# A hybrid attention and state-space layer on one core: the first pairs' products in another order, and norms, table load and splits queued in another place

## The chip, the cores and the metric

The kernel runs on one core of a Trainium2 chip. The metric is the device time of one execution in microseconds. A core has TensorE (PE in the profile, its weight loads PEld), VectorE (DVE), ScalarE (ACT), GpSimd (POOL) and SyncE (SP), which issues most of the transfers. Each engine works through its own queue in order and waits on semaphores for the others.

## The reference

One decoder layer on x of 1024 rows by 1024 columns, float32. What matters here is the head of it: the normalised input and one combined projection.

```python
def _rmsnorm(x, g):
    xf = x.astype(jnp.float32)
    y = xf * lax.rsqrt(jnp.mean(xf * xf, axis=-1, keepdims=True) + RMS_EPS) * g.astype(jnp.float32)
    return y.astype(x.dtype)
...
    h = _rmsnorm(x, pre_g)
    proj = jnp.einsum('bld,de->ble', h, w_in)
    z_ssm, xbc, dt_raw, q, k, v, f_raw, z_att, g_ssm, g_att = jnp.split(proj, _offsets(IN_SPLITS), axis=-1)
```

A state-space branch and an attention branch follow, are gated and merged, go through `w_out`, are normalised and added to x. The change touches none of these.

## The kernel before

Every large product is done in pairs of 128 output columns, by a scheme of seven half-size products in place of eight. A `Pair` holds two column tiles of weights, each in two halves of rows (`a11`, `a12`, `a21`, `a22`). `Pair.do(which)` runs product 1 to 7: twelve matmuls of 128x512, three for each of four row tiles, since each operand is kept as a high part (`h`) and the rest (`l`) and h·h, h·l and l·h are added. `OPERAND` names the moving operand of each product: 1 takes `b11` (tiles `x0h`, `x0l`), 2 `b21` (`x1`), 6 `-t2` (`x4`), 5 `t1` (`x3`), 7 `t3` (`x5`), 4 `t4` (`x6`), 3 `-b22` (`x2`). Products 1, 6, 7 and 4 of a pair add up in one PSUM bank (`pb`; p and q, the first two pairs, have one each), 5 and 3 use the bank `pc`, which all pairs share, and 2 uses `pd`. After 1, 6 and 7 ScalarE copies the bank (`s`, L402); `give` (L406 to L416) then makes the four results on VectorE or ScalarE.

`prepare` makes the weights of a product three steps ahead: sums of quarters (`sum`, L355, L371) and the split of a sum or of a raw tile into two parts (`wop`: the high one on ScalarE, L349, the rest on VectorE, L350). The list `Stream.steps` sets the order of products; `half()` runs half of one. Raw tiles (`raw`, six buffers) are loaded through SyncE as soon as the weights made from the old ones are prepared.

Ahead of the stream stands the start (from L1143). Eight tiles of x, 128x1024 each, are loaded. `norm_tiles` squares each (ScalarE, or VectorE for tiles 1 and 3), takes the root on ScalarE (L1175) and the reciprocal on VectorE, and scales the tile: the first four on VectorE (L1178), the other four on GpSimd (L1180). A first loop over eight column blocks turns the first four tiles on TensorE (`pt`), scales them out of PSUM into `low`, and splits `low` into `x0` and `x1` with `put`; from the fifth block on, half a product runs behind each. The second loop has four blocks (j): eight turns of the other four tiles, two copies out of PSUM on ScalarE (`up`, and `b`, both L1225), eight passes of `df` (the columns of dt and f), the differences `t1`, `t2` and their splits `x3`, `x4`, half of a product 2, and two more differences into `low` (L1239, L1240). After it `low` is split into `x5` (`t3`) and `x6` (`t4`), and `b` into `x2` (`-b22`).

`summing` is a small 128x64 matrix by which `df` is turned (`pt_df`), the first work of the state-space stage; behind it a chain of small VectorE operations makes dt (L689 to L713).

What orders this: a scheduler places the instructions of each engine by a timeline of its own. `mm`, `turn` and `pin` keep program order; `tc.high_priority()` puts work ahead; `tc.issue_after(op)` puts it behind `op` on the engine's queue.

Of the kernel before, what the change touches and what calls it, by code (L numbers as in the profile page):

```python
# [16 lines left out]
P = 128  # L17
T = 1024
D = 1024
NK = D // P  # L20
KH = NK // 2
# [65 lines left out]
def hybrid_layer(ctx: ExitStack, tc, a, out):  # L87

    nc = tc.nc
# [5 lines left out]
    ident = const.tile([P, P], F32, name="ident")  # L95
# [6 lines left out]
    epst = const.tile([P, 1], F32, name="epst")  # L102
# [33 lines left out]
    def small(name="th"):  # L136
        return gp.tile([P, HALF], F32, tag="th", name=name)
# [21 lines left out]
    class Operands:  # L159
# [298 lines left out]
    class Stream:  # L458
# [6 lines left out]
        def __init__(self, pairs, double, last):  # L465
            self.pairs = pairs
            for n, p in enumerate(pairs):
                p.bank, p.other = (pj, "be"[n % 2]), (pjx, "d") if n < double else (pj, "c")

                p.between = n < double or n >= last  # L470

            p, q, r = pairs[0:3]
            self.steps = [(p, 1), (q, 1), (p, 2), (q, 2)] + [(p, n) for n in (6, 5, 7, 4, 3)]
            self.steps += [(q, 6), (q, 5), (q, 7), (r, 1), (q, 4), (q, 3)]
            for n in range(2, last):
                p, nxt = pairs[n], pairs[n + 1]
                self.steps += [(p, i) for i in ((2, 6, 5, 7) if n < double else (6, 2, 7, 5))] + [(nxt, 1)]
                self.steps += [(p, 4), (p, 3)] if n + 1 < last else [(p, 3), (p, 4)]

            a, b, c, d, e, f, g, h = pairs[last:]  # L480
            self.steps += [(a, 5), (a, 6), (a, 7), (b, 1), (a, 2), (a, 4), (a, 3)]
            for p, nxt in ((b, c), (c, d), (d, e)):
                self.steps += [(p, 2), (p, 6), (p, 5), (p, 7), (nxt, 1), (p, 4), (p, 3)]
            self.steps += [(f, 1), (e, 2), (e, 6), (e, 5), (e, 7), (f, 2), (e, 4), (e, 3)]
            self.steps += [(f, 6), (f, 5), (f, 7), (g, 1), (f, 4), (f, 3)]
            self.steps += [(g, 2), (g, 6), (g, 5), (g, 7), (h, 1), (g, 4), (g, 3)]
            self.steps += [(h, 6), (h, 5), (h, 7), (h, 2), (h, 3), (h, 4)]
            self.following = {p: n.ops for p, n in zip(pairs, pairs[1:]) if n.ops is not p.ops}
            self.building = []
            self.chores, self.line = [], []  # L490
            self.held = None
            self.count = 0
            self.at = 0
            self.run = None
            self.waiting = []
            self.loads = [(p, names) for p in pairs for names in (("a11", "a12"), ("a21", "a22"))]
            self.loaded = []
            self.load_next()
# [19 lines left out]
        def begin(self):  # L518
            self.load_next()
            self.load_next()  # L520
            for p, which in self.steps[:3]:
                self.prepare(p, which)

        def prepare(self, p, which):
# [69 lines left out]
        def ahead(self, after):  # L594

            if self.at + 3 < len(self.steps):
                p, which = self.steps[self.at + 3]
                if after == (p.keys[0][0] == "merged"):
                    self.prepare(p, which)

# [442 lines left out]
    order = [p for ps in by_group for p in ps]  # L1043
# [100 lines left out]
    with tc.tile_pool(name="pro", bufs=1, reuse_waits="tile", side="right") as pro, tc.tile_pool(  # L1144
        name="prop", bufs=1, space=PSUM, reuse_waits="tile", side="right"
# [5 lines left out]
        ss = pro.tile([P, NT], F32, name="ss")  # L1151
        rstd = pro.tile([P, NT], F32, name="rstd")
        low = pro.tile([P, NK, HALF], F32, name="low")
# [11 lines left out]
                tiles.append(xt)  # L1165
            return tiles

        def norm_tiles(hf, tiles):
            for t, xt in enumerate(tiles, 4 * hf):
                sqt = small("sqt").bitcast(BF16)  # L1170
                if t in (1, 3):
                    nc.vector.tensor_tensor_reduce(sqt, xt, xt, 1.0, 0.0, ALU.mult, ALU.add, ss[:, t : t + 1])
                else:
                    nc.scalar.activation(sqt, xt, AF.Square, accum_out=ss[:, t : t + 1])
                nc.scalar.activation(rstd[:, t : t + 1], ss[:, t : t + 1], AF.Sqrt, bias=epst, scale=1.0 / D)  # L1175
                nc.vector.reciprocal(rstd[:, t : t + 1], rstd[:, t : t + 1])
                if hf == 0:
                    nc.vector.tensor_scalar(xt, xt, rstd[:, t : t + 1], None, ALU.mult)  # L1178
                else:
                    nc.gpsimd.tensor_scalar(xt, xt, rstd[:, t : t + 1], None, ALU.mult)  # L1180

        def turned(tiles, k):
            pt = prop.tile([P, HALF], F32, tag="pt", bufs=2, name="pt")
            for j in range(4):
                turn(pt[:, j * P : (j + 1) * P], tiles[j][:, k * P : (k + 1) * P]) 
            return pt
# [9 lines left out]

        tiles = load_tiles(0)
        stream = Stream(order + late + ends, len(order) + 3, len(order) + len(late) + 4)
        norm_tiles(0, tiles)
        tiles2 = load_tiles(1)  # L1200
        stream.begin()
        for k in range(NK):
            pt = turned(tiles, k)
            if k > 1:
                nc.scalar.activation(low[:, k, :], pt, AF.Copy, scale=preg[:, k : k + 1])
            else:
                nc.vector.tensor_scalar(low[:, k, :], pt, preg[:, k : k + 1], None, ALU.mult)
            put("b11" if k < KH else "b21", k % KH, low[:, k, :])
            if k >= KH:
                stream.halves(1)  # L1210
        norm_tiles(1, tiles2)

        for k, h in [(k, h) for j in range(KH) for k, h in ((j, 0), (j + KH, 0), (j + KH, 1))]:
            pin(nc.sync.dma_start(wo_dram[k, :, half(h)], a["wo"][k * P : (k + 1) * P, half(h)]))
# [1 line left out]
        b22 = []  # L1216
        for j in range(KH):
            up = []
            if j % 2 == 0:
                two = pro.tile([P, D], F32, tag="xt", bufs=6, name="b22")  # L1220
                b22 += [two[:, 0:HALF], two[:, HALF:D]]
            for k in (j, j + KH):
                pt = turned(tiles2, k)
                up.append(b22[j] if k >= KH else pro.tile([P, HALF], F32, tag="up", bufs=1, name="up"))
                nc.scalar.activation(up[-1], pt, AF.Copy, scale=preg[:, k : k + 1])  # L1225
            b11, b21 = low[:, j, :], low[:, j + KH, :]
            for n, (k, m) in enumerate(((j, b11), (j, up[0]), (j + KH, b21), (j + KH, up[1]))):
                mm(df[32 * n : 32 * n + 32, :], wdf[:, k, :], m, start=(j == 0), stop=(j == KH - 1))
            with tc.high_priority():
                t1 = small()  # L1230
                nc.vector.tensor_tensor(t1, up[0], b11, ALU.subtract)
                put("t1", j, t1)
                t2 = small()
                nc.vector.tensor_tensor(t2, up[1], t1, ALU.subtract)
                last = put("-t2", j, t2, -1.0)
            stream.halves(1)

            with tc.issue_after(last[1]) if j == KH - 1 else nullcontext():
                nc.vector.tensor_tensor(b11, t2, b11, ALU.subtract)  # L1239
                nc.vector.tensor_tensor(b21, t2, b21, ALU.subtract)  # L1240
        dft = small("dft")
        nc.scalar.activation(dft, df, AF.Identity, bias=bdf)
        stream.halves(1)
# [1 line left out]
        with tc.issue_after(last[0]), tc.issue_after(last[1]):  # L1245
            for j in range(KH):
                put("t3", j, low[:, j, :], order=pin)
        stream.halves(1)
        early.close()
        pools["t4"] = phase_a.enter_context(tc.tile_pool(name="xp4", bufs=1, reuse_waits="tile"))  # L1250
        xop["t4"] = place(pools["t4"], "t4")
        for j in range(KH):
            put("t4", j, low[:, j + KH, :], order=pin)
        stream.halves(1)
        for j in range(KH):
            put("-b22", j, b22[j], -1.0, order=pin)
        stream.halves(5)


    with tc.tile_pool(name="ssm", bufs=1, reuse_waits="tile", side="right") as sp, tc.tile_pool(  # L1260
        name="ssmp", bufs=1, space=PSUM, reuse_waits="tile", side="right"
# [14 lines left out]
        ng = cst[:, 88:96]  # L1276
        dsk = cst[:, 96:104]
        alog = cst[:, 104:120]

        summing = sp.tile([P, 4, P], F32, tag="ce", bufs=1, name="summing")[:, 0, 0:64]  # L1280
        nc.vector.tensor_tensor(summing, ident[:, 0:64], ident[:, 64:P], ALU.add)

        nc.vector.tensor_scalar(cst[:, 0:80], cst[:, 0:80], 0.5, None, ALU.mult)
        dtn = sp.tile([P, NT, 32], F32, name="dtn")
# [19 lines left out]
    with tc.tile_pool(name="att", bufs=1, reuse_waits="tile", side="right") as ap, tc.tile_pool(  # L1304
        name="attp", bufs=1, space=PSUM, reuse_waits="tile", side="right"
# [23 lines left out]
        q, k, v, fb = {}, {}, {}, {}  # L1329
# [331 lines left out]
        made = []  # L1661
        for m in range(6 * NK + 1):
# [36 lines left out]
            made = turned(hp, g, list(end(m - 1)))  # L1699
# [70 lines left out]
```

## Time and profile before

| | us |
|---|---|
| three runs: median (lowest to highest) | 1277.65 (1277.15 to 1278.29) |
| the profiled execution, its own time | 1276.47 |
| its span (first to last instruction) | 1274.7 |
| busy in the span: TensorE | 1246.8 |
| VectorE | 1013.5 |
| ScalarE | 795.3 |
| GpSimd | 325.8 |

Busy is the time in which an engine had an instruction at work. A row of the timeline gives start, length, engine, line, operation, what it writes and reads, and in brackets how long the engine was idle before it and what ended that. The chain of waits is followed back from the last instruction of a stretch: at each step to what released it, or to the instruction before it on its engine. Rows of groups end with the count, the busy time and the mean in ns.

### The profile page before, as it was taken

To read this page: it belongs to the slowest core of one execution; us is meant where nothing else is said; L and a number is where in the kernel's file an instruction comes from. 1 tells how busy PE (TensorE), PEld (TensorE's weight loads), DVE (VectorE), ACT (ScalarE), POOL (GpSimd) and SP (SyncE) were. 2 spreads that over 40 slices of the span, in tenths; PEclk is the share of its full clock that TensorE was granted. 3 is DMA by queue.
4 is the path that set the end of the run, shared out by engine and by line. 5 is a ranking of instruction groups with operands and counts; after the bars stand their busy time and mean duration, and the time that the engine had idled before them with its cause. 6 is when DMAs were issued, how large, how long until landed. Compare 5 with 4: busy or idle time off the path is not lost.

```text
span 1274.7 us, 20831 instructions
## 1 busy us (share of the span) xinstructions
PE 1246.8 (98%) x6926; PEld 982.8 (77%) x6926; DVE 1013.5 (80%) x1994; ACT 795.3 (62%) x1738; POOL 325.8 (26%) x338
## 2 busy tenths in 40 slices
PE   5999999999999999999999999999999999999997
PEld 3688888887888888888887777777777777778886
DVE  7988886988888978997877676767689767886975
ACT  7745665556665765566555666666687666844754
POOL 4000440013400241114222123223112212356062
PEclk9999999999999999999999999999999999999999
DMA  8233552646336533644456466666688657766932
GB/s 296 71 121 73 143 168 89 191 147 196 126 104 216 174 121 119 218 147 140 140 162 241 164 233 200 218 211 221 232 282 275 214 185 250 252 214 198 364 114 100
DMA packets 151212, 233.56 MB, mean 183 GB/s; under 512 B 15201, under 2 KB 60737, under 8 KB 151105
## 3 DMA queue, kind: packets, MB, share of 16 engines
q1 hardware_dynamic: 133760, 191.89, 46.9%
q0 software_dynamic: 6784, 22.29, 4.6%
q10 hardware_dynamic: 10560, 18.06, 3.8%
q8 instruction: 54, 0.88, 0.3%
q14 instruction: 54, 0.43, 0.1%
HBM read 162.99 MB, written 72.34 MB: 185 GB/s over the span
## 4 chain that ended last, share of the span: by engine, by line
PE 78%; DVE 7%; DMA 6%; ACT 5%; issue 2%; SPq 0%; POOL 0%; DVEq 0%; ACTq 0%; POOLq 0%
PE pb L128 33%; PE pc L128 19%; PE pd L128 6%; PE av L128 5%; PE pt L131 4%; PE s L128 4%; PE yps L128 2%; DVE wop L350 1%; DMA xt<-in_x 1%; PE st L128 1%; DVE sum L355 1%; DMA rb<-st_dram 1%; ACT ex L1486 1%; PE tr L131 1%; ACT wop L349 1%
## 5 line engine op out<-in xcount | busy, mean ns | idle before, releaser
L350 DVE TENSOR_TENSOR wop<-sum,wop 128x512 fp32r<-128x512 f32 x180 | 140.0, 779 | 51.2 <-ACT wop L349 50.2
L349 ACT ACTIVATE wop<-sum 128x512 fp32r<-128x512 f32 x180 | 112.5, 626 | 107.6 <-DVE sum L355 53.7
L1486 ACT ACTIVATE ex<-ex,nm 128x512 f32<-128x512 f32 (+1 forms) x192 | 116.2, 606 | 71.4 <-DVE nm L1482 71.1
L402 ACT ACTIVATE s<-pb 128x512 f32<-128x512 f32 x144 | 85.3, 592 | 94.5 <-PE pb L128 92.2
L128 PE MATMUL pb<-x0h,wop 128*128 128x512 f32 x384 | 131.7, 400 | 0.0
L128 PE MATMUL pc<-x3h,wop 128*128 128x512 f32 x384 | 129.8, 396 | 1.1 <-DVE th L412 0.8
L128 PE MATMUL pb<-x5h,wop 128*128 128x512 f32 x384 | 130.1, 396 | 0.7 <-ACT s L402 0.7
L128 PE MATMUL pb<-x6h,wop 128*128 128x512 f32 x384 | 129.5, 395 | 1.3 <-ACT s L402 1.3
L128 PE MATMUL pc<-x2h,wop 128*128 128x512 f32 x384 | 130.3, 397 | 0.0
L350 DVE TENSOR_TENSOR wop<-raw,wop 128x512 fp32r<-128x512 f32 x144 | 105.8, 736 | 30.4 <-ACT wop L349 30.3
L128 PE MATMUL pb<-x4h,wop 128*128 128x512 f32 x384 | 129.1, 395 | 0.0
L1482 DVE CUSTOM_DVE_ANT_0 ex<-s,fb 128x512 f32<-128x512 f32 (+1 forms) x192 | 96.9, 552 | 19.0 <-PE s L128 15.1
L349 ACT ACTIVATE wop<-raw 128x512 fp32r<-128x512 f32 x144 | 89.7, 623 | 14.9 <-PE pd L128 6.2
L128 PE MATMUL pd<-x1h,wop 128*128 128x512 f32 x288 | 96.4, 394 | 0.0
L128 PEld LDWEIGHTS pb<-x6h,wop 128*128 128x128 f32 x384 | 72.1, 188 | 18.5 <-issue 2.1
L128 PEld LDWEIGHTS pb<-x5h,wop 128*128 128x128 f32 x384 | 72.1, 188 | 18.5 <-issue 2.0
L128 PEld LDWEIGHTS pb<-x0h,wop 128*128 128x128 f32 x384 | 72.7, 189 | 17.6 <-issue 2.9
L128 PEld LDWEIGHTS pc<-x3h,wop 128*128 128x128 f32 x384 | 72.1, 188 | 18.3 <-issue 1.5
L128 PEld LDWEIGHTS pc<-x2h,wop 128*128 128x128 f32 x384 | 72.1, 188 | 17.3 <-issue 2.4
L128 PEld LDWEIGHTS pb<-x4h,wop 128*128 128x128 f32 x384 | 72.1, 188 | 16.7 <-issue 1.9
L211 POOL TENSOR_TENSOR wd<-wd 128x256 f32<-128x256 f32 x32 | 31.8, 994 | 202.0 <-DMA wd<-in_wo 131.6
L131 PE MATMUL pt<-ident,ex 128*128 128x128 f32 x576 | 75.2, 273 | 2.2 <-ACT ex L1486 1.5
(314 smaller groups left out, 3002.2 us busy)
## 6 DMA issues: line engine op xcount, KB each, us to landing
raw<-in_wu SPq DMA_DIRECT2D x128, 256.0 KB
csb<-cs_dram SPq DMA_DIRECT2D x32, 256.0 KB
q<-q_dram SPq DMA_DIRECT2D x32, 256.0 KB
k<-k_dram SPq DMA_DIRECT2D x16, 512.0 KB
fb<-f_dram SPq DMA_DIRECT2D x16, 512.0 KB
rb<-st_dram SPq DMA_DIRECT2D x48, 128.0 KB
wd<-in_wo SPq DMA_DIRECT2D x40, 128.0 KB
xt<-in_x SPq DMA_DIRECT2D x8, 512.0 KB
```

The costliest lines, as they stand in the source:

```text
L128: return tc.keep_in_program_order(nc.tensor.matmul(*args, **kw))
L131: return tc.keep_in_program_order(nc.tensor.transpose(out_, in_, idn))
L211: pin(nc.gpsimd.tensor_tensor(t[out_], t[a_], t[b_], ALU.subtract))
L349: nc.scalar.activation(op[:, 0], src, AF.Copy)
L350: nc.vector.tensor_tensor(op[:, 1], src, op[:, 0], ALU.subtract)
L355: self.adds.tensor_tensor(t, x, y, ALU.add)
L402: nc.scalar.activation(s, ps, AF.Copy)
L1482: nc.vector.tensor_tensor_reduce(o, s[e][:, 0:w], fb[hp, h][:, e, 0:w], 1.0, 3.0e38, ALU.add, ALU.min, nm)
L1486: pin(nc.scalar.activation(o, o, AF.Exp, scale=-1.0, bias=nm, accum_out=hd.at(hd.sm, i, h, e)))
```

## The change

Six things are changed.

- Of the first two pairs, p and q, the products after p's 7 come in another order: q's 6, then p's 3, then p's 4, where p's 4 and 3 and then q's 6 stood. The weights of p's 3 are made before those of q's 6 (`order`).
- The norms of tiles 0 to 3 have priority, and the first weights' splits are queued behind the last root and the last scaling of them. Tile 2 is scaled on ScalarE.
- Tiles 4 to 7 are normed in pieces: 4 and 5 after the first loop in program order, 6 behind the split of the fifth block's `x1l`, 7 behind that of the sixth; tile 7 is scaled on VectorE.
- In the first loop the half products are queued behind the split.
- The subtraction that makes `t4` (L1240) goes from VectorE to GpSimd.
- `-b22` is split ahead of `t4`, and `summing` is made in a tile of the common ring at the end of the start.

```diff
             p, q, r = pairs[0:3]
-            self.steps = [(p, 1), (q, 1), (p, 2), (q, 2)] + [(p, n) for n in (6, 5, 7, 4, 3)]
-            self.steps += [(q, 6), (q, 5), (q, 7), (r, 1), (q, 4), (q, 3)]
+            self.steps = [(p, 1), (q, 1), (p, 2), (q, 2), (p, 6), (p, 5), (p, 7), (q, 6), (p, 3), (p, 4)]
+            self.steps += [(q, 5), (q, 7), (r, 1), (q, 4), (q, 3)]
...
+            self.order = list(self.steps)
+            self.order[7:9] = self.order[8], self.order[7]
...
-            for p, which in self.steps[:3]:
+            for p, which in self.order[:3]:
                 self.prepare(p, which)
...
-                p, which = self.steps[self.at + 3]
+                p, which = self.order[self.at + 3]
...
-        def norm_tiles(hf, tiles):
-            for t, xt in enumerate(tiles, 4 * hf):
+        def norm_tiles(tiles, t0):
+            hf, scaled = t0 // 4, None
+            for t, xt in enumerate(tiles, t0):
                 sqt = small("sqt").bitcast(BF16)
...
-                nc.scalar.activation(rstd[:, t : t + 1], ss[:, t : t + 1], AF.Sqrt, bias=epst, scale=1.0 / D)
+                root = nc.scalar.activation(rstd[:, t : t + 1], ss[:, t : t + 1], AF.Sqrt, bias=epst, scale=1.0 / D)
                 nc.vector.reciprocal(rstd[:, t : t + 1], rstd[:, t : t + 1])
-                if hf == 0:
-                    nc.vector.tensor_scalar(xt, xt, rstd[:, t : t + 1], None, ALU.mult)
+                if t == 2:
+                    nc.scalar.activation(xt, xt, AF.Copy, scale=rstd[:, t : t + 1])
+                elif hf == 0 or t == 7:
+                    scaled = nc.vector.tensor_scalar(xt, xt, rstd[:, t : t + 1], None, ALU.mult)
                 else:
                     nc.gpsimd.tensor_scalar(xt, xt, rstd[:, t : t + 1], None, ALU.mult)
+            return root.ins, scaled and scaled.ins
...
-        norm_tiles(0, tiles)
+        with tc.high_priority():
+            root, scaled = norm_tiles(tiles, 0)
         tiles2 = load_tiles(1)
-        stream.begin()
+        with tc.issue_after(root), tc.issue_after(scaled):
+            stream.begin()
+        made = []
         for k in range(NK):
...
-            put("b11" if k < KH else "b21", k % KH, low[:, k, :])
+            made.append(put("b11" if k < KH else "b21", k % KH, low[:, k, :]))
             if k >= KH:
-                stream.halves(1)
-        norm_tiles(1, tiles2)
+                with tc.issue_after(made[-1][1]):
+                    stream.halves(1)
+        norm_tiles(tiles2[:2], 4)
+        for t in (6, 7):
+            with tc.issue_after(made[t - 4][0]), tc.issue_after(made[t - 2][1]):
+                norm_tiles(tiles2[t - 4 : t - 3], t)
...
-                nc.vector.tensor_tensor(b21, t2, b21, ALU.subtract)
+                nc.gpsimd.tensor_tensor(b21, t2, b21, ALU.subtract)
...
+        stream.halves(1)
+        for j in range(KH):
+            put("-b22", j, b22[j], -1.0, order=pin)
         stream.halves(1)
         early.close()
...
-        stream.halves(1)
-        for j in range(KH):
-            put("-b22", j, b22[j], -1.0, order=pin)
         stream.halves(5)
+        summing = small("summing")[:, 0:64]
+        nc.vector.tensor_tensor(summing, ident[:, 0:64], ident[:, 64:P], ALU.add)
```

What the scheduler makes of it shows in each engine's order. ScalarE, in the second loop, from the second block's end to the last block's copies (`up` and `b` are the two copies out of PSUM of a block, `b_419` that of the last two blocks; `th` under the table load is the tanh of the first gate). Before:

```order
L349 ACTIVATE wop<-sum 128x512
L1225 ACTIVATE up<-pt,preg 128x512
L1225 ACTIVATE b_419<-pt,preg 128x512
L626 ACT_TABLE_LOAD
L626 ACTIVATE th<-th 128x512
L627 DMA gs_dram<-th 128x512
L1190 ACTIVATE x3h<-th 128x512
L1225 ACTIVATE up<-pt,preg 128x512
L1225 ACTIVATE b_419<-pt,preg 128x512
L1190 ACTIVATE x4h<-th 128x512
```

And now (L1238, L628 and L1196 are the same lines under new numbers):

```order
L349 ACTIVATE wop<-sum 128x512
L1196 ACTIVATE x4h<-th 128x512
L1238 ACTIVATE up<-pt,preg 128x512
L628 ACT_TABLE_LOAD
L628 ACTIVATE th<-th 128x512
L1238 ACTIVATE b_419<-pt,preg 128x512
L629 DMA gs_dram<-th 128x512
L1196 ACTIVATE x3h<-th 128x512
L1238 ACTIVATE up<-pt,preg 128x512
L1196 ACTIVATE x4h<-th 128x512
L1238 ACTIVATE b_419<-pt,preg 128x512
```

The load and the tanh now stand between a block's two copies, and an `x4h` ahead of the third block's first copy and of the last block's second.

VectorE, from the splits of the last operands to `summing` (`x2l`, `x5l`, `x6l` are the low parts of `-b22`, `t3`, `t4`; `th L414` is p's fourth result). Before:

```order
L1192 TENSOR_TENSOR x6l<-low,x6h 128x512 x3
L350 TENSOR_TENSOR wop<-sum,wop 128x512
L1194 TENSOR_SCALAR x2l<-b_344,x2h 128x512
L1192 TENSOR_TENSOR x6l<-low,x6h 128x512
L1194 TENSOR_SCALAR x2l<-b_344,x2h 128x512
L1194 TENSOR_SCALAR x2l<-b_419,x2h 128x512
L355 TENSOR_TENSOR sum<-sum,raw 128x512
L1194 TENSOR_SCALAR x2l<-b_419,x2h 128x512
L414 TENSOR_TENSOR th<-pc,s 128x512
L1265 MEMSET onesr 128x128
L1281 TENSOR_TENSOR summing<-ident 128x64
```

And now:

```order
L1200 TENSOR_SCALAR x2l<-b_344,x2h 128x512 x2
L1200 TENSOR_SCALAR x2l<-b_419,x2h 128x512 x2
L350 TENSOR_TENSOR wop<-sum,wop 128x512
L371 TENSOR_TENSOR sum<-sum,raw 128x512
L1198 TENSOR_TENSOR x6l<-low,x6h 128x512 x4
L350 TENSOR_TENSOR wop<-raw,wop 128x512
L414 TENSOR_TENSOR th<-pc,s 128x512
L1272 TENSOR_TENSOR summing<-ident 128x64
```

`x2l` now comes ahead of `x6l`, a sum and a raw split have come in, and `summing` is still last.

VectorE behind `summing`, up to `th L416`, p's third result, which empties the bank `pc`. Before:

```order
L684 COPY t<-pt_df 128x128 x2
L355 TENSOR_TENSOR sum<-raw 128x512
L689 TENSOR_SCALAR t<-t 128x256
L350 TENSOR_TENSOR wop<-sum,wop 128x512
L416 TENSOR_TENSOR th<-s,pc 128x512
L692 TENSOR_SCALAR t<-t 128x256
```

And now (L686, L691, L694 to L696 are L684, L689, L692 to L694 of before):

```order
L686 COPY t<-pt_df 128x128 x2
L691 TENSOR_SCALAR t<-t 128x256
L350 TENSOR_TENSOR wop<-sum,wop 128x512
L694 TENSOR_SCALAR t<-t 128x256
L695 RECIPROCAL t<-t 128x256
L355 TENSOR_TENSOR sum<-raw 128x512
L696 TENSOR_TENSOR t<-t 128x256
L416 TENSOR_TENSOR th<-s,pc 128x512
```

The reciprocal, a sum and a small operation now stand ahead of `th L416`; on TensorE p's product 4 now lies between p's product 3, which fills that bank, and q's 5, which needs it.

More of the change, by code (lines that the diff above doesn't have):

```diff
@@ L1278, in hybrid_layer @@
         alog = cst[:, 104:120]
-        summing = sp.tile([P, 4, P], F32, tag="ce", bufs=1, name="summing")[:, 0, 0:64]
-        nc.vector.tensor_tensor(summing, ident[:, 0:64], ident[:, 64:P], ALU.add)
         nc.vector.tensor_scalar(cst[:, 0:80], cst[:, 0:80], 0.5, None, ALU.mult)
```

## The prediction

> **What bounds the kernel now.** I read the page's first two parts first. TensorE is busy for 98% of the span and at full clock in every slice; only the first two of the 40 slices are not full. So the change, whose rows all stand in the first 90 us, can only move the moment from which TensorE runs without gaps. Then the chain of waits for the first 70 us, in order of time, with start, length, engine, tile and line:
>
> ```profile
> 6.39 5.95 DMA xt<-in_x
> 12.37 1.16 ACT sqt L1174 x2
> ...
> 20.57 1.04 ACT wop L349 x2
> ...
> 28.70 0.58 ACT up L1225
> 29.32 1.62 PE df L128 x6
> ...
> 44.35 1.59 PE pd L128 x6
> 45.97 0.69 DVE th L412
> ...
> 49.67 1.80 DVE x5l L1192 x3
> ...
> 59.58 1.10 PE pt_df L128 x8
> 60.68 2.81 PE pc L128 x12
> 63.49 2.72 PE pb L128 x12
> ```
>
> Four stretches follow each other. Input tiles arrive until 12.37. ScalarE then works without a pause until the first `up` at 28.6. The four blocks of the second loop (eight turns, `df`, half a product) are paced by TensorE and what it asks of ScalarE until 45.8. VectorE sets the pace from 45.97 until `summing`, at 0.60 us per 128x512 operation (three `x5l` in 1.80). After `pt_df` the timeline names no wait of TensorE up to 160 us, and the order of every engine from about 90 us on is the one before. A shift of `pt_df`, and any new wait behind it, therefore stays to the end.
>
> **The start.** In the changed order ScalarE's first load is for the squares, and the load for the roots stands behind the first square. Rows of the timeline:
>
> ```profile
> 5.03 1.06 ACT L1174 ACTIVATE sqt<-xt 128x1024 bf16<-128x1024 f32 x1 [1.35 <-DMA xt<-in_x]
> ...
> 12.03 0.75 DVE L1178 TENSOR_SCALAR xt<-xt,rstd 128x1024 f32<-128x1024 f32 x1
> ...
> 12.37 1.06 ACT L1174 ACTIVATE sqt<-xt 128x1024 bf16<-128x1024 f32 x1 [1.12 <-DMA xt<-in_x]
> ...
> 13.36 0.75 DVE L1207 TENSOR_SCALAR low<-pt,preg 128x512 f32<-128x512 f32 x1 [0.57 <-PE pt L131]
> ...
> 14.28 8.50 POOL L1180 TENSOR_SCALAR xt<-xt,rstd 128x1024 f32<-128x1024 f32 x3 [12.92 <-DVE rstd L1176]
> ...
> 22.78 0.64 ACT L1190 ACTIVATE x1h<-low 128x512 fp32r<-128x512 f32 x1
> ...
> 23.57 3.74 POOL L1180 TENSOR_SCALAR xt<-xt,rstd 128x1024 f32<-128x1024 f32 x1 [0.79 <-DVE rstd L1176]
> ...
> 23.99 0.68 DVE L1192 TENSOR_TENSOR x1l<-low,x1h 128x512 fp32r<-128x512 f32 x1
> ...
> 28.58 0.70 ACT L1225 ACTIVATE up<-pt,preg 128x512 f32<-128x512 f32 x1
> ```
>
> The new load (1.28 us, row below) delays the first root by about 1.5 us. Against that the fourth tile's scaling no longer waits behind the first weights' split, and the third tile's is ScalarE's. Walked through, the fourth scaling starts near 11.6 instead of 12.03 and the first `low` near 12.9 instead of 13.36. That is just enough: ScalarE must wait for the fifth tile at 12.37 anyway, and comes to the first `x0h` at about 13.7. The load is hidden by ScalarE's waits of 1.35 and 1.12 us; without that cover it would cost its 1.3.
>
> From 12.37 ScalarE has the same list to do before the first `up`, less two splits of sums (`wop`, 0.52 each) that now stand behind it: 28.58 - 1.04 = 27.5. But the seventh tile's reciprocal is now queued on VectorE behind the first `x1l`, and GpSimd scales that tile afterwards. I place `x1h` at 22.6 (one `low` more, one `wop` and one root less ahead of it). `x1l` follows at about 23.4, as two weight splits still stand ahead of it. Its 0.68 and the reciprocal and its handover, 0.25, put GpSimd's start at 24.3. GpSimd's earlier three rows took 2.83 each, the last 3.74, with VectorE working beside it nearly without a pause. The tile is ready at 27.1 or at 28.0, and `up` follows 0.5 later (the remaining turns), at 27.6 or 28.5. VectorE is as busy then as beside the last row, so I take 28.3: **-0.3 us** (-1.0 to +0.1).
>
> **The blocks.** The third block's rows:
>
> ```profile
> 37.05 0.63 ACT L349 ACTIVATE wop<-sum 128x512 fp32r<-128x512 f32 x1 [1.03 <-PE pd L128]
> ...
> 37.59 0.67 ACT L1225 ACTIVATE up<-pt,preg 128x512 f32<-128x512 f32 x1
> ...
> 38.16 0.68 ACT L1225 ACTIVATE b<-pt,preg 128x512 f32<-128x512 f32 x1
> ...
> 38.85 1.28 ACT L626 ACT_TABLE_LOAD   x1
> ...
> 38.89 0.14 PEld L128 LDWEIGHTS df<-b,wdf 128*32 128x32 f32 x2 [0.43 <-ACT b L1225]
> ...
> 39.86 0.50 PE L128 MATMUL pd<-x1h,wop 128*128 128x512 f32 x1
> ...
> 40.15 0.63 ACT L626 ACTIVATE th<-th 128x512 f32<-128x512 f32 x1
> ...
> 41.99 0.69 ACT L1225 ACTIVATE up<-pt,preg 128x512 f32<-128x512 f32 x1
> ...
> 42.58 0.68 ACT L1225 ACTIVATE b<-pt,preg 128x512 f32<-128x512 f32 x1
> ```
>
> Before, `b` follows `up` and the table load for the tanh comes behind both; TensorE's `df<-b` starts 0.05 after `b` ends, having waited for it. Now an `x4h` stands between the split (which waits for the product's end at 37.05) and `up`: `up` starts at 38.1 instead of 37.59. Then come the load and the tanh, and only then `b`. `up` ends at 38.78, the load takes until 40.08 (38.85 to 40.15 before, 1.30), the tanh 0.52, so `b` starts at 40.6 instead of 38.16: **+2.4 us** (2.0 to 2.6; 1.9 if the `x4h` finds room). Behind `b` on TensorE's queue are `df<-b`, half a product and all the turns of the last block; nothing there can go ahead of it. In the last block an `x4h` comes between `up` and `b`, which were 0.59 apart: **+0.5 us** (0.4 to 0.6). The four subtractions moved to GpSimd (1.48 each, row below) take 2.4 us off VectorE, three of them where it waits for TensorE, about 1.3 us a block; the start of each is free and the last is needed only by the product that now comes later.
>
> [...]
>
> **VectorE's stretch.** It starts with `th L412`, which waits for the second half product, and every one of the following operations stands behind it. Before, 22 intervals and `onesr` lie between it and `summing`; now 22, since what went (a subtraction, an `x3l`) made room for a sum and a split. 22 x 0.603 = 13.27.
>
> ```profile
> 59.37 0.15 DVE L1281 TENSOR_TENSOR summing<-ident 128x64 f32<-128x64 f32 x1
> ...
> 62.54 0.41 DVE L689 SCALAR_TENSOR_TENSOR t<-t 128x256 f32<-128x256 f32 x1
> ...
> 63.92 0.68 DVE L416 TENSOR_TENSOR th<-s,pc 128x512 f32<-128x512 f32 x1
> ...
> 66.05 0.39 PE L128 MATMUL pc<-x3h,wop 128*128 128x512 f32 x1
> ...
> 66.36 0.69 DVE L355 TENSOR_TENSOR sum<-raw 128x512 f32<-128x512 f32 x1 [0.96 <-DMA raw<-in_wu]
> 66.97 1.75 DVE L693 RECIPROCAL t<-t 128x256 f32<-128x256 f32 x1
> ...
> L884 POOL TENSOR_TENSOR ce<-ce,ct 128x512 f32<-128x512 f32 x28 | 41.5, 1482 | 31.6 <-ACT ce L883 31.6
> ```
>
> Before it was 59.37 - 45.97 = 13.40, so **-0.1 us**. The new order of the products removes TensorE's wait of 1.3 us for the copy of product 7, but TensorE then stands before `pt_df`, which still needs `summing`. It would come to it about 2 us early; that gain is lost in VectorE's queue.
>
> **Behind it.** q's product 5 (`pc<-x3h`, 66.05 before) reuses the bank that `th L416` empties. Before, `th L416` ran at 63.92, well ahead. Now it stands behind the reciprocal (1.67 to the next start) and a `sum` that waits for a load. From its start I count: `summing` 0.15, split 0.6, memsets 0.15, `cst` 0.2, sum 0.6, copies and L689's operation 0.8, a split that waits for ScalarE 0.6, 0.2, reciprocal 1.67, sum 0.6 and its neighbour 0.45, `th` 0.68, and about 0.3 of waiting: 7.0. TensorE came to q's product 5 66.05 - 59.37 = 6.7 after that start, behind `pt_df` and two products. **+0.3 us** (0 if all is early). The load is issued behind the first sum, 2.4 after `summing`; before, one issued after 62.95 was there at 66.33, 3.4 later, which puts its sum at 5.8 at best; if the load is slower by 2 us, so is the product. The upper end is +2.3.
>
> **Sum:** -0.3 + 2.4 + 0.5 - 0.1 + 0.3 = +2.8 us. The profiled execution took 1276.47 us, 1.8 of it around the span, and would take 1279.3. The median of the runs is 1277.65, 1.2 above it; I give 1280.5 on that scale.
>
> **The rivals.**
> *Faster (7%): VectorE is no longer the bound.* If `summing` is done before TensorE has finished q's product 6, the stretch is TensorE's own, four products of 2.72: `pt_df` at 45.77 + 10.9 = 56.7 instead of 59.58, -2.9. With the blocks' delay paid it comes to -0.3 + 2.4 + 0.5 - 2.9 = -0.3, no change; with that delay covered as well, to 1277.65 - 0.3 - 2.9 = 1274.5. The point of decision is whether those two `b` reach TensorE on time. For it speak the 2.4 us taken off VectorE, against it the order, in which all 22 operations are behind `th L412` and the load ahead of `b`.
> *No change that can be told (23%): GpSimd takes 2.83.* The start gives -1.0, q's product 5 doesn't wait: -1.0 + 2.4 + 0.5 - 0.1 = +1.8, 1279.5. For it speak three of four rows. Here I also count that a later wait of TensorE takes the delay up; against that, its timeline shows none to 160 us.
> *Slower still (20%): the load for r's second half is late* and q's product 5 waits 2 us more: 1282.5. For it speaks the wait of 0.96 for the same kind of load.
> *VectorE stands still while GpSimd scales the seventh tile (6%).* Then the second `x1l` waits from 25.0 to 27.1, the eighth tile, now VectorE's, is scaled by 28.7 and `up` starts at 29.2: +0.6 instead of -0.3, 1281.4. [...]
> *Forecast, 44%.*
>
> **How the numbers follow.** About 0.2%, 2.55 us, is what can be told from no change here. Slower by more: the forecast, the late load and the standstill, 0.70. Within: 0.23. Faster: 0.07. The forecast lies close to that border, which the two cases beyond it make likelier to be passed than not. The range: the bounds of the terms add to -1.0 + 1.9 + 0.4 - 0.2 = +1.1 and +0.1 + 2.6 + 0.6 + 2.3 = +5.6; I take 1278.3 to 1283.0, which leaves out the faster case and the far ends.
>
> **What would show it.** In the new profile: ScalarE's first `up` near 28.3; in the third block a load and a tanh between `up` and `b`, and TensorE waiting about 2 us for `b`; the second half product's end near 48.4; VectorE without a pause from there to `summing` near 61.9; `pt_df` after it, with TensorE waiting some 2 us for `summing`; a wait for `th L416` near 68.5. It is wrong if `pt_df` starts before 60, or if TensorE waits anywhere after 75.

## The result, and the profile after

| | before | after |
|---|---|---|
| median of the runs, us | 1277.97 (1275.30 to 1278.43) | 1284.37 (1282.97 to 1285.06) |
| profiled execution: time, span | 1276.47, 1274.7 | 1285.06, 1283.3 |
| start of q's product 5 in it | 66.21 | 73.63 |

The change costs 6.4 us: the ratio is 1.0047, with an interval of 1.0033 to 1.0061. 1280.5 was forecast, and 1283.0 was the upper end of the range.

Below is the chain of waits of the changed kernel (start, length, engine, tile, line). Lines have moved: L1238 was L1225 (`up`, `b`), L1244 and L1247 were L1231 and L1234 (the differences), L1252 and L1253 were L1239 and L1240, L628 was L626 (the gate's tanh).

```profile
28.77 0.60 DVE sum L355
...
34.26 0.60 DVE wop L350
34.86 0.60 DVE x3l L1198
35.46 0.60 DVE sum L371
36.07 0.60 DVE x4l L1200
36.67 0.60 DVE sum L355
37.27 0.61 DVE th L1244
...
39.48 0.67 ACT up L1238
...
40.17 1.28 ACT L628
...
41.46 0.63 ACT th L628
42.09 0.59 ACT b L1238
...
42.72 1.92 PE df L128 x2
44.64 2.12 PE pd L128 x6
...
51.73 0.69 DVE th L412
...
65.38 1.20 PE pt_df L128 x8
66.57 4.31 PE pc L128 x12
70.89 2.74 PE pb L128 x12
73.63 2.72 PE pc L128 x12
```

Set it beside the chain of the kernel before. From 28.8 VectorE leads, where ScalarE and TensorE did; its sums and splits of weights stand ahead of the second block's first difference (`th L1244`, 37.27 in the chain, 37.19 in the timeline). Before, this difference started at 33.88:

```profile
33.88 0.68 DVE L1231 TENSOR_TENSOR th<-up,low 128x512 f32<-128x512 f32 x1
```

In the changed kernel ScalarE's `x3h` waits for it, and `wop`, `x4h` and `up` stand behind `x3h` on ScalarE's queue:

```profile
37.91 0.63 ACT L1196 ACTIVATE x3h<-th 128x512 fp32r<-128x512 f32 x1 [3.55 <-DVE th L1244]
```

The third block's `up` starts at 39.48 instead of 37.59, and `b`, behind the load and the tanh, at 42.0 instead of 38.16. `th L412` is 5.76 late. From there to `summing` it takes 13.38, as before (13.40). Then p's product 3 takes 4.31, where a product took 2.72 to 2.81, and q's product 5 is 7.42 late. The span has grown by 8.6; the other 1.2 lies in small waits after 300 us, which differ from run to run: TensorE's waits of 0.15 us and more after 100 us add to 6.3 here and to 4.9 before. The medians differ by less, 6.4: the profiled run of the change is the slowest of its six, and that of the kernel before lies below its median.

The two products that take too long are matters of the clock. TensorE's rows, with the idle time ahead of them in brackets, and the view by windows of 1 us (length, TensorE's busy time, granted clock, DMA):

```profile
42.72 1.92 PE L128 MATMUL df<-b,wdf 128*32 128x512 f32 x2 [1.47 <-ACT b L1238]
...
65.38 1.20 PE L128 MATMUL pt_df<-summing,dft 128*128 128x64 f32 x8 [1.88 <-DVE summing L1272]
```

```profile
42.00:43.00 1.00, 0.28 (x1) 0.68 0.03 10
43.00:44.00 1.00, 1.00 (x2) 0.50 0.65 252
44.00:45.00 1.00, 1.00 (x2) 0.50 0.00 0
45.00:46.00 1.00, 1.00 (x4) 0.61 0.00 0
...
66.00:67.00 1.00, 1.00 (x7) 0.63 0.70 264
67.00:68.00 1.00, 1.00 (x4) 0.50 0.64 215
68.00:69.00 1.00, 1.00 (x3) 0.50 0.87 207
69.00:70.00 1.00, 1.00 (x4) 0.67 0.80 295
```

The clock is halved twice. What is missing to 1.00 adds to 1.71 and 1.70 us, so each drop lasts 3.4 us and costs up to 1.7 of work. The profile of the kernel before shows 1.00 in every stretch of 2 us from 28 to 100 us. The last section sets drops beside the waits ahead of them.

So the 7.4 us of this profile are: 1.9 for `up`, 1.95 for load and tanh, 1.4 for the clock in the third block, 0.5 for the last block, and 1.6 for the clock in p's product 3 and `pt_df`.

### The profile page after: what moved, and what is told of

Read it like the earlier page. It is cut to its first block, busy times and chain, and to the rows that moved or that the text cites. A ratio compares the mean times of both kernels' runs of the same rounds, so it can differ in the third digit from the quotient of the medians.

```text
span 1283.3 us, 20834 instructions
## 1 busy us (share of the span) xinstructions
PE 1251.2 (97%) x6926; PEld 985.1 (77%) x6926; DVE 1012.4 (79%) x1990; ACT 797.5 (62%) x1740; POOL 330.2 (26%) x341
## 4 chain that ended last, share of the span: by engine, by line
PE 81%; DMA 6%; DVE 5%; ACT 3%; issue 3%; POOL 1%; SPq 0%; DVEq 0%; ACTq 0%; POOLq 0%
PE pb L128 35%; PE pc L128 20%; PE pd L128 7%; PE av L128 4%; PE pt L131 4%; PE s L128 4%; PE yps L128 2%; DMA xt<-in_x 1%; DMA wo_dram<-in_wo 1%; PE st L128 1%; PE tr L131 1%; PE tr_v L131 1%; DMA fb<-f_dram 1%; DMA rb<-st_dram 1%; DVE wop L350 1%
## 5 line engine op out<-in xcount | busy, mean ns | idle before, releaser
L879 POOL TENSOR_TENSOR xe<-xdt,tend 128x256 f32<-128x256 f32 x28 | 26.1, 931 | 197.8 <-DVE xdt L847 193.6
```

Of the source, the lines that this page charges most:

```text
L879: nc.gpsimd.tensor_tensor(xe, s["xdt"], tend[:, c, hs].unsqueeze(2).to_broadcast([P, 4, 64]), ALU.mult)
```

## The experiments

The theory after the result: the first loop's sums, queued behind the splits, come due among the differences of the second loop and make VectorE the bound there; what else is lost (load ahead of `b`, half clock) follows from that place in the order. The main rival: GpSimd's subtraction holds VectorE up. Of each run, q's product 5 in the profile is compared with 66.21, and the time with the kernel before on the same chip.

| run | q's product 5 | ratio (interval) |
|---|---|---|
| the change | 73.63 | 1.0047 (1.0033 to 1.0061) |
| e1, sums free | 67.78 | 1.0014 (1.0002 to 1.0027) |
| e2, load behind `b` | 70.53 | 1.0038 (1.0025 to 1.0051) |
| e3, t4 on VectorE | 66.97 | 1.0004 (0.9992 to 1.0017) |
| e4, wait filled | 70.33 | 1.0041 (1.0025 to 1.0056) |
| e5, products alone | 72.05 | 1.0037 (1.0021 to 1.0053) |
| e6, e1 and e3 | 65.93 | 1.0000 (0.9988 to 1.0012) |
| e7, t4 late | 65.96 | 1.0046 (1.0028 to 1.0064) |
| e8, e7 and e3 | 65.75 | 1.0048 (1.0031 to 1.0065) |
| e9, norms alone | 66.63 | 1.0012 (0.9999 to 1.0024) |
| e10, halves alone | 68.54 | 1.0009 (0.9997 to 1.0020) |
| e11, GpSimd alone | 68.00 | 1.0016 (1.0002 to 1.0030) |
| e12, the change again | 73.08 | 1.0047 (1.0033 to 1.0061) |

### e1: the sums back in the first loop

```diff
-                with tc.issue_after(made[-1][1]):
-                    stream.halves(1)
+                stream.halves(1)
```

> The changed kernel, but the half products of the first loop (and with them the sums and splits of weights that they call for) are not queued behind the split. Theory 'late sums': in the changed kernel these sums stand on VectorE among the differences of the second loop, so the second block's first difference comes at 37.2 instead of 33.9 and the third block's first copy at 39.5 instead of 37.6; with the sums back in the first loop the third block's first copy comes near 37.6, the load of the tanh's table stands behind the second copy, th L412 of the second half product comes near 46.0 instead of 51.7, and the time is 5.8 us less than the changed kernel's 1284.4: 1278.6 (1277.5 to 1279.7), with TensorE still waiting for summing and still at a lower clock behind that wait. Rival 'standstill': GpSimd's subtractions, which are still there, hold VectorE up; then the third block's first copy is still over 1 us late and the time is 1281 to 1282.5.

ScalarE's rows of this run, and one of VectorE's with GpSimd's beside it:

```profile
37.59 0.67 ACT L1237 ACTIVATE up<-pt,preg 128x512 f32<-128x512 f32 x1
38.16 0.68 ACT L1237 ACTIVATE b<-pt,preg 128x512 f32<-128x512 f32 x1
38.86 1.28 ACT L628 ACT_TABLE_LOAD   x1
```

```profile
36.39 1.59 POOL L1252 TENSOR_TENSOR low<-th,low 128x512 f32<-128x512 f32 x1 [2.69 <-DVE th L1246]
```

```profile
36.76 1.77 DVE L1251 TENSOR_TENSOR low<-th,low 128x512 f32<-128x512 f32 x1
38.45 0.68 DVE L412 TENSOR_TENSOR th<-pd,s 128x512 f32<-128x512 f32 x1
```

`up` and `b` are where they were before the change, to 0.01 us, with the load behind them: in the changed kernel, taking out the one `issue_after` is enough for all of that. `th L412` of the second half product starts at 46.16. The rival is wrong about `up` but right that VectorE is held up: its operation beside GpSimd's row takes 1.77 instead of 0.68 and ends at 38.53, 0.55 after GpSimd's row (to 37.98). In this run it happens once a block (1.76, 1.77, 1.76 and 1.50): VectorE is spared 0.60 a block and loses 0.8 to 1.1. With the last such standstill, behind `th L412`, and one more split, `summing` comes 14.7 after `th L412` instead of 13.4; with the 0.19 ahead of `th L412` that is 1.5 of the 1.57 us that are left. The ratio is 0.0033 below the change's, 4.2 us, and the two intervals do not meet; 5.8 was expected, of which the trace shows 5.85.

### e2: the load behind `b`

The first gate's tanh is kept back and queued behind the third block's `b`:

```diff
...
-                nc.scalar.activation(up[-1], pt, AF.Copy, scale=preg[:, k : k + 1])
+                copied = nc.scalar.activation(up[-1], pt, AF.Copy, scale=preg[:, k : k + 1])
+            if held:
+                with tc.issue_after(copied.ins):
+                    held.pop()()
```

> The changed kernel, but the table load and the tanh of the first gate are queued behind the third block's second copy. Theory 'late sums': the load is worth its own 1.95 us, the x4h that also falls behind the last block's second copy 0.5, and the half clock that follows TensorE's two waits up to 1.4; the third block's first copy stays at 39.5. 1280.6 to 1282.0. Rival 'the load alone': as the prediction priced it, nearly all of the loss comes from the load's place, and the time returns to within 1 us of the kernel before, 1277.5 to 1279.

The third block's `up` stays late (39.40), `th L412` comes at 47.79 instead of 51.73: 3.9 for the load, the clock and the last block's `x4h`, as the theory had it. But q's product 5 is still 4.3 late, and the time is 4.9 us above the kernel before (0.0038 of it), where "the load alone" allows 1 and the theory 2.6 to 4.0. By its time alone this run is not told from the change, whose interval it overlaps; the rows tell it. 1.6 of the 4.3 is VectorE's stretch, as in e1; and 0.86 is a wait for `th L416`, behind a sum whose load landed late: the prediction's rival of the late load, which the change itself does not show.

### e3: the subtraction back on VectorE

```diff
-                nc.gpsimd.tensor_tensor(b21, t2, b21, ALU.subtract)
+                nc.vector.tensor_tensor(b21, t2, b21, ALU.subtract)
```

> The changed kernel, but the subtraction that makes t4 is on VectorE again; the order that follows also has the load behind the second copy and summing ahead of the split of t4. Theory 'late sums': the sums still stand among the differences, so the third block's first copy is still 1 us or more late (38.6 to 39.5), but the load's place is gone and TensorE no longer waits for summing: 1276.5 to 1279. Rival 'standstill': without GpSimd's subtractions VectorE is on time and the third block's first copy comes at 37.6 to 38.0.

`th L1244` of the second block starts at 36.96 (37.19 with the change, 34.77 in e1) and `up` at 38.73: the sums are worth 2.4 us of VectorE there, the subtraction's move 0.2, or 0.5 counted from each run's own first `up` (28.84 here, 28.60 with the change). That tells the two theories apart. But with this one line changed the scheduler puts the load behind `b` and `summing` ahead of `t4`'s splits, and so product 5 comes at 66.97. In time this undoes nearly all of the change; the rows, not the time, show why.

### e4: the wait ahead of `pt_df` filled

```diff
         pt = pp.tile([P, HALF], F32, tag="tr", bufs=2, name="pt_df")
+        xh = xop["b11"][0]
+        for _ in range(8):
+            mm(pt, xh[:, 0, 0:P], xh[:, 0, :], start=True, stop=True)
```

> The changed kernel, with eight extra matmuls of 128x512 on TensorE in the wait ahead of pt_df, into the tile that pt_df then overwrites: 8 x 0.23 = 1.8 us of work in a wait of 1.9. Theory 'half clock after a wait': the product behind pt_df takes 4.3 us in the changed kernel, because the granted clock is 0.5 there; with the wait filled it takes 2.7 to 2.9 and the granted clock is 1.00, and the time is 1.5 us less than the changed kernel's: 1282.9. Rival: the product is slow for another reason (loads, its operands), stays at 4.3, and the time stays at 1284.4 or grows by a part of the extra work.

The extra products are overwritten by `pt_df`; nothing is left out. In the chain of this run p's product 3 takes its usual time:

```profile
63.69 1.10 PE pt_df L128 x8
64.79 2.82 PE pc L128 x12
```

And its third block, with the same two waits as the change, has no drop either:

```profile
39.91 0.62 PE L128 MATMUL df<-up,wdf 128*32 128x512 f32 x1 [1.33 <-ACT up L1241]
...
42.43 1.04 PE L128 MATMUL df<-b,wdf 128*32 128x512 f32 x2 [1.47 <-ACT b L1241]
```

So the drop is not a fixed price of those waits, and the run can't be read as proof that the filling removed the second one. The median is 0.8 us below the change's by the ratios, 1.5 was expected; the intervals overlap.

### e5 to e8: the products' order, and whether a faster version is there

e5 is the kernel before with `steps` and `order` of the change, and nothing else. e6 is e1 and e3 together. e7 is e1 with `summing` made at the start and this edit, e8 is e7 with e3:

```diff
...
+        stream.halves(3)
         for j in range(KH):
             put("t4", j, low[:, j + KH, :], order=pin)
-        stream.halves(5)
...
+        stream.halves(2)
```

> The kernel before, with only the products of p and q in the new order. Theory: the new order frees TensorE of its wait for the copy of product 7, but summing then stands 23 operations of VectorE behind th L412, at 45.97 + 23 x 0.60 = 59.9; TensorE reaches pt_df near 56.8 and waits 3 us for it, so pt_df starts near 60.0 instead of 59.58. Behind it th L416 stands behind the reciprocal and q's product 5 waits for it, near 67.2 instead of 66.2. Time 1 to 3 us more than before: 1279.6 to 1281.6, the upper end if the clock halves in that wait. Rival 'the order of the products is a gain by itself': pt_df starts before 59 and the time is 1 to 3 us less than before.

> The changed kernel with both: the half products not queued behind the split, and t4's subtraction on VectorE. Theory: the standstills of 1.08 us per block (one VectorE operation takes 1.76 instead of 0.68 beside GpSimd's subtraction) are gone, th L412 starts at 45.97, summing comes 18 operations later, at 57.0, just when TensorE gets to pt_df; pt_df starts near 57.5 instead of 59.58 in the kernel before, and the time is 1 to 2 us less than before's. Rival 'GpSimd relieved VectorE': VectorE has four operations of 0.6 more and th L412 or summing comes later than with the first of these edits alone (60.9), so the time is no better than that kernel's ratio of 1.0014.

> The changed kernel with the half products not queued behind the split, summing made at the start, and t4's splits behind product 7's result; the subtraction stays on GpSimd. Theory: TensorE is the bound from the second half product to q's product 5, but for 0.8 us that VectorE stands still beside GpSimd's last subtraction. pt_df at 57 to 58, the product behind it at once, q's product 5 at 63.7 to 65.5 (66.2 in the kernel before): the time is 1 to 2.5 us less than before's. Rival: the splits moved back now hold up p's product 4, or th L416 comes late, and the time is within 1 us of before's or more.

> As the one before, with t4's subtraction on VectorE as well. Theory: no standstill, pt_df near 57, q's product 5 near 64; 1.5 to 2.5 us less than the kernel before. Rival as before, and 'GpSimd relieved VectorE': then this is slower than the run with the subtraction on GpSimd.

e5 was worse than expected. VectorE's row of the load, and TensorE's:

```profile
66.92 0.69 DVE L355 TENSOR_TENSOR sum<-raw 128x512 f32<-128x512 f32 x1 [2.33 <-DMA raw<-in_wu]
```

```profile
72.05 0.76 PE L128 MATMUL pc<-x3h,wop 128*128 128x512 f32 x1 [3.64 <-DVE th L416]
```

`pt_df` starts at 61.78 (60.0 expected), TensorE having waited 2.46 us for `summing`; then the sum waits for its load, the reciprocal and `th L416` stand behind it, and q's product 5 waits 3.64 and takes 5.46 instead of 2.72, at a granted clock of 0.50 from 72 to 78 us. The new order of the products alone is no gain: it moves the wait for the copy to the two waits behind. The median is 4.7 us above the kernel before (0.0037 of it), where 1 to 3 were expected.

e6 has no standstill in the second loop: all of VectorE's operations of 128x512 take 0.68 or 0.69 there. `summing` comes 11.4 after `th L412`, and `pt_df` starts at 59.55; product 5 is 0.28 earlier than before the change, where 1 to 2 were expected, since q's product 6 waits 1.18 for its weights' split. "GpSimd relieved VectorE" is refuted: with the subtraction back, product 5 comes 1.85 us earlier than in e1.

e7 and e8 reach product 5 at 65.96 and 65.75, about when e6 does, where 63.7 to 65.5 and about 64 were expected: `pt_df` starts at 59.6 and 59.4, since TensorE waits for splits on the way (1.30 and 0.58 in e7, 0.32 and 1.18 in e8). And they are as slow as the change. Their next wait is at `pt_te`, the first product that needs dt. The row of e7, and then those of the kernel before:

```profile
89.29 0.55 PE L128 MATMUL pt_te<-da,stri 128*128 128x128 f32 x1 [4.29 <-DVE da L715]
```

```profile
84.10 0.28 DVE L713 SCALAR_TENSOR_TENSOR da<-dtn,ea 128x128 f32<-128x128 f32 x1
...
85.09 0.39 PE L128 MATMUL pt_te<-da,stri 128*128 128x128 f32 x2
```

Before the change the chain of small operations that makes dt is done 0.7 us before TensorE comes to it. Whatever TensorE gains at 60 us beyond that, it waits out at 85, unless that chain moves too, and it does move with VectorE's order: it is done at 82.36 in e1, at 85.84 in e6, and only at 89.14 and 88.93 in e7 and e8. In these two the four `x6l` that the edit moved stand on VectorE ahead of the copies of `pt_df`, which come at 64.06 in e7 instead of 61.54; that is 2.5 of the 4.8 us there. TensorE waits 1.02 at `pt_te` in e6 and 4.29 in e7 and e8, and in these the granted clock then falls to 0.50, for 6.8 us in e7 and 3.4 in e8. No version here has both an early `pt_df` and an early dt, and none beats the kernel before.

### e9 to e11: one part of the change on the kernel before

The edits are those of the change: the norms in e9; in e10 `with tc.issue_after(made[1])` around the first loop's `stream.halves(1)`; in e11 `nc.gpsimd` for the subtraction.

> The kernel before, with only the norms changed (priority and order of the first four, tile 2 on ScalarE, tiles 4 to 7 in pieces, tile 7 on VectorE). Theory: the start is worth nothing; the first copy of the second loop comes within 0.5 us of 28.58, no load is misplaced, and the time is within 1.2 us of before's. Rival, the prediction's term: it comes at 27.6 to 28.3 and TensorE's second loop starts 0.3 to 1.0 us earlier.

> The kernel before, with only the first loop's half products queued behind the split; nothing is on GpSimd but the norms, and the load of the tanh's table stays behind the second copy. Theory 'late sums': four sums and two splits that were done before 28.6 now stand among the differences, so the second block's first difference comes 1.5 to 2.5 us later than 33.88, the third block's first copy 1 to 2 us later than 37.59, and the time is 1 to 2 us more than before's, more where the clock halves. Rival: VectorE has room there (it waits 0.4 to 0.5 us a block for TensorE) and the third block's first copy stays within 0.5 us of 37.59.

> The kernel before, with only the subtraction for t4 on GpSimd. Theory 'standstill': in each block one VectorE operation takes about 1.7 us instead of 0.68, as long as GpSimd's row lasts, so VectorE loses 1.08 where it saves 0.60; the last of the four falls behind th L412, and pt_df starts 0.2 to 0.9 us later than 59.58. Time 0 to 1.5 us more than before's. Rival, the prediction's term: GpSimd takes 0.6 us a block off VectorE, all operations keep 0.68, and pt_df starts 0.4 to 0.6 us earlier.

e9: the first `up` starts at 28.43 (28.58 before), product 5 0.4 later. No gain from the norms shows; the interval reaches from none to a loss of 3 us.

e10: the first `up` starts at 29.85, the third block's at 39.90, 2.3 late where 1 to 2 were expected; the time is 1.1 us longer, with an interval that includes no change. The reason is another than expected: here the scheduler puts the sums ahead of the first difference, so the second block's first difference is only 1.17 late (35.05), as late as the start itself, and the other 1.0 is ScalarE's order (an `x4h` ahead of the second block's `b`, and one ahead of `up`). The place of the sums among the differences needs the other parts too.

e11: four operations take 1.77, 1.78, 1.76 and 1.19 us; `pt_df` starts at 59.41, 0.17 earlier: between the two expectations, since an operation less stands in the stretch. Behind `summing` the order has changed, too: the reciprocal and a `sum` that waits 1.05 for its load stand ahead of `th L416`, q's product 5 waits 1.95 and the granted clock is 0.52 from 69 to 72 us.

### e12: the change, profiled again

> The changed kernel as it is, profiled a second time. Theory: the waits of TensorE (1.32 and 1.47 us in the third block, 1.88 ahead of pt_df) come from the order and are the same to 0.2 us; whether the granted clock halves after them is not fixed by the order (the run with the filled wait had the same two waits in its third block and kept 1.00). So q's product 5 starts at 73.6 if both drops are there, near 72.2 or 72.1 with one, and near 70.7 with none. Rival: the drops follow from the waits alone and stand at the same two places again, with product 5 at 73.6.

The chain of this run:

```profile
42.65 1.91 PE df L128 x2
44.56 2.86 PE pd L128 x6
47.42 1.71 PE pt L131 x8
49.13 0.99 PE df L128 x6
...
52.82 0.69 DVE th L412
...
66.47 1.10 PE pt_df L128 x8
67.57 2.79 PE pc L128 x12
```

The waits are the same (1.32, 1.47, 1.89), the drops are not: the first lasts 6.8 us instead of 3.4, and `th L412` is 1.1 later; the second is missing, and p's product 3 takes 2.79. Product 5 starts at 73.08. Neither expectation fits in full: the order does not fix where a drop comes, as the theory said, nor its length, which the theory had not said.

## Why the prediction was wrong

- **The start (-0.3).** Measured 0.0: `up` at 28.60. GpSimd's scaling of the seventh tile took 3.15, between the two cases of 2.83 and 3.74, but it did not set `up`: the eighth tile's scaling, moved to VectorE, took 1.63 instead of 0.75 and ended 0.5 later. The rival of the standstill had the right place (the second `x1l` took 1.33 instead of 0.68) and too high a price: no run shows the wait of 2.1 (25.0 to 27.1) that it counted; this `x1l` was 0.65 longer.
- **The third block (+2.4).** This is the first of two steps that failed. "`up` starts at 38.1 instead of 37.59" took the split ahead of it to wait for the product's end at 37.05, as before. But ScalarE's queue has the second block's `x3h` ahead of that split, and this waits for `th L1244`. VectorE's list from 28 to 38 was never added up: up to that difference it holds three sums, one split and two `x1l` more than before, and one standstill. Measured: 39.48, 1.4 more, and `b` 3.8 late. From `up` to `b` the step was right: 2.5 forecast and measured.
- **The four subtractions, "2.4 us off VectorE".** Beside the first of them one VectorE operation took 1.76, beside the second 1.45, so 1.85 of the 2.4 were lost again, and the 1.08 of the first fell ahead of the difference that `up` waited for; in e1 all four cost VectorE 4.1. The prediction quoted GpSimd's 1.48 and did not ask what VectorE does meanwhile. In the rows of the change, e1 and e11 VectorE's operation takes 1.19 to 1.78 against 0.68 beside GpSimd's, or GpSimd's takes longer instead (2.21 in the change's third block, against 1.58 in the first, with VectorE's two at 0.68).
- **The last block (+0.5)** and **VectorE's stretch (-0.1)** held: 0.5, and 13.38 against 13.40.
- **No term for the clock.** This is the second step that failed. The prediction forecast a wait of about 2 us for `b` and of some 2 for `summing` (1.47 and 1.88 measured), and let TensorE go on at full clock behind them. Measured: 1.4 and 1.6 in the first profile, about 2.5 and 0 in the second. What it costs in the mean of many runs can be estimated from their granted clocks: 0.9963 over the changed kernel's twelve runs, 0.9981 over 91 runs of the kernel before. The difference is 0.0018 of 1280 us, 2.3 us.
- **Behind it (+0.3).** Measured 0: `th L416` started at 71.05 and was done 6.6 behind `summing`'s start, where 7.0 was counted. The half clock ahead of product 5 is not the reason: in e12, without it, TensorE did not wait there either. The late load is real: in e2, e5 and e11 the `sum` waits 0.86, 2.33 and 1.05 for it, and TensorE 0.86, 3.64 and 1.95 for the `th L416` behind.
- **The rivals.** "Faster", 1274.5, left out the dt chain: it had 0.7 us to spare at 85 us before, and in e3, e6, e7 and e8 TensorE waits 1.0 to 4.3 for it. Whether it could have come with another order is open: in e1 the chain is done 2.0 earlier than before. "Slower still" named another cause than the one that came; that its 1282.5 lies nearer to the result is luck.
- **The range.** The lower bounds add to 1277.65 + 1.1 = 1278.75, so 1278.3 is not their sum. And of the page's 40 slices for TensorE the first and the last are not full, not the first two; nothing hangs on either.

The terms add to 0.0 + 3.8 + 0.5 + 0.0 + 0.0 = 4.3 without the clock, where 2.8 was forecast, and to 7.3 with the first profile's 3.0 for it; with the 2.3 of the mean they add to 6.6, and the medians show 6.4. Neither step alone would have led out of the range: 1277.65 + 4.3 is 1282.0, and 1280.5 + 2.3 is 1282.8. What stays open is why the scheduler places the sums and the load as it does, and what decides whether the clock drops.

## What to carry to other kernels

When a change queues work behind something, add up that engine's whole list in the stretch where the work now falls, and follow each wait back through the queue of the engine that waits: what stands ahead there may wait for something else. Before moving an operation to GpSimd, look in the trace for VectorE's rows beside GpSimd's two-input rows: if one of them takes GpSimd's whole time, as here 1.77 instead of 0.68 beside a row of 1.59, nothing is saved. A new wait on TensorE can cost more than its length, as here 1.88 and then 3.4 us at half clock, and a gain ahead of a chain that is only just in time is worth no more than that chain's margin.

## What the runs showed that was not expected

The length of a wait does not tell whether TensorE's clock drops behind it. Below are waits of TensorE and the stretch in which the granted clock is 0.50 there (in e4 the rows have their usual length, 1.04 for the two passes behind the second wait against 1.92 in the change):

| profile | TensorE's waits, us | end of the last one | clock 0.50 from | for, us |
|---|---|---|---|---|
| the change, third block | 1.32, 1.47 | 42.72 | 42.4 | 3.4 |
| e12, third block | 1.32, 1.47 | 42.65 | 42.2 | 6.8 |
| e4, third block | 1.33, 1.47 | 42.43 | no drop | |
| the change, `pt_df` | 1.88 | 65.38 | 66.2 | 3.4 |
| e12, `pt_df` | 1.89 | 66.47 | no drop | |
| e5, `pt_df` | 2.46 | 61.78 | no drop | |
| e11, product 5 | 1.95 | 68.00 | 68.5 | 3.4 |
| e5, product 5 | 3.64 | 72.05 | 71.2 | 6.8 |
| e7, `pt_te` | 4.29 | 89.29 | 88.1 | 6.8 |
| e8, `pt_te` | 4.29 | 89.08 | 89.4 | 3.4 |
| e8, late | 1.69 | 1122.60 | 1123.6 | 3.4 |
| e7, late | 0.77, 0.16 | 1114.87 | 1115.5 | 3.4 |

The same two waits in the third block are followed by a drop of 3.4 us, by one of 6.8 and by none; 1.88 ahead of `pt_df` is followed by one, 1.89 and 2.46 are not. Some drops start while TensorE still waits, others behind the wait. What starts a drop, and what sets its length, these runs do not show, and no run was made to test it.

Beside GpSimd's subtraction (two inputs) either engine's row can be the longer one: in the change VectorE's operation took 1.76 in the second loop's first block, beside GpSimd's 1.58, and in the third block GpSimd's row at 44.39 took 2.21 while VectorE's two operations beside it took 0.68 each. Which of them waits was not tested. Beside GpSimd's one-input scalings the rows are mixed: in the change, inside the row at 24.49 (3.15), one `x1l` took 1.33, and the scaling of a tile that VectorE began in it 1.63 (0.75 for the one at 11.41), while in the kernel before, inside the row at 23.57 (3.74), `x1l` took its usual 0.68 and a split 1.09:

```profile
25.11 1.33 DVE L1198 TENSOR_TENSOR x1l<-low,x1h 128x512 fp32r<-128x512 f32 x1 [0.19 <-ACT x1h L1196]
```
